# Eight of 22 feature blocks of the down projection as seven products in place of eight, with weight sums formed by adding transfers

## The chip, the cores and the metric

One core of one Trainium2 chip runs the whole layer. The metric is the device time of one execution in microseconds (us); lower is better. TensorE (PE) multiplies matrices, and its weight loads are shown apart as PEld. VectorE (DVE), ScalarE (ACT) and GpSimd (POOL) do elementwise work. SyncE (SP) and POOL issue the DMA transfers, each from a queue of its own.

## The reference

One decoder layer on 256 tokens with 2048 features, in float32:

```python
h = rmsnorm(x, attn_norm_g)
proj = h @ w_in                      # split among two attention groups
x = x + concat([o_mla, o_nsa]) @ w_o
h = rmsnorm(x, ffn_norm_g)
x = x + (silu(h @ w_gate) * (h @ w_up)) @ w_down   # 5632 hidden features
return rmsnorm(x, final_norm_g)
```

The change concerns the product with `w_down`, a 5632 x 2048 matrix: 44 blocks of 128 hidden features by 4 groups of 512 output columns.

## The kernel before

**Weights.** A class `Stream` brings every weight tile of 128 x 1024 from HBM, in the order in which PE uses them. `_dma` issues the load from SP's queue into one of three buffers (`wraw`). `_split` makes two parts of it: ACT casts it to a rounded copy `whi` (line 142), and DVE subtracts that from the tile to get the rest, `wlo` (line 144). While `W.share` is 256, in the attention stage and the output projection, POOL subtracts the last 256 columns (line 146) and DVE the first 768. Each of `whi` and `wlo` has three buffers, and `get` splits up to two tiles ahead of the one that PE uses. A product of two split operands takes three matmuls: high by high, high by low, low by high.

**The feed-forward stage.** The 44 feature blocks are worked in two halves of 22 (`h` is 0 or 1). For each block, `gate_up` multiplies two tiles of the gate and two of the up weights, 128 features at a time, into two PSUM banks (tags `ds` and `PT`, two buffers each). `activate` turns them into the split activation `aT`: copies by ACT, additions by DVE, one multiplication by POOL, the SiLU by ACT.

Then the half's down projection runs over four column groups `dg`. For each, 11 tiles of two feature blocks are multiplied with token half 0 and token half 1 into two banks (`down`, lines 863 to 865); one tile is 12 matmuls of 512 columns:

```python
for k in range(2):
    nc.tensor.matmul(pt, h_, wh, ...)   # activation high, weight high
    nc.tensor.matmul(pt, h_, wl, ...)
    nc.tensor.matmul(pt, l_, wh, ...)
```

After each group, DVE adds the two banks to `x`.

**The end.** In the last group (`h` 1, `dg` 3) the last four weight tiles are held back for token half 1. Token half 0 is added, normalized and stored while PE works the held tiles in two column halves of 256 (banks `dnh0`, `dnh1`; 48 matmuls of 256 columns). After the last of them come an addition of 256 columns by DVE, a sum of squares by ACT, a small reduction, a power by POOL, the scaling by DVE and ACT, and four stores by SP.

**Order of instructions.** PE executes in the order of the program text (`program()` writes it out by hand). The other engines and the DMA queues get an order that a planner makes from its estimates when the kernel is built: among the instructions whose inputs and buffers are free by the plan, the earlier in the text goes first. Where a wait is needed, a queue waits in that order.

Of the kernel before, what the change touches and what calls it, by code (L numbers as in the profile page):

```python
# [30 lines left out]
NSA_SCALE = 0.125  # L31


def program():
# [45 lines left out]
    for h in range(2):  # L80
        for f in range(h * NFH, (h + 1) * NFH):
            if f == 0:
                s += w(("gate", 0, 0), ("up", 0, 0)) + [("tp", 3)] + w(("gate", 1, 0), ("up", 1, 0))
                s += [("rb2",)] + w(("gate", 0, 1), ("up", 0, 1), ("gate", 1, 1), ("up", 1, 1))
            elif f > 1:
                s += w(*A("gate", f), *A("up", f))
        s += [("w", ("down", h, dg, j)) for dg in range(4) for j in range(NFH // 2)]
    return s


def plan():

    return [k[1] for k in program() if k[0] == "w"]
# [6 lines left out]
class Stream:  # L100
# [3 lines left out]
    SPLIT_AHEAD = 2  # L104

    def __init__(self, nc, pool, order, src):
        self.nc, self.pool, self.order, self.src = nc, pool, order, src
        self.raw, self.done = {}, {}
        self.nd = self.ns = self.nu = 0
        self.cuts = {0: (0, 368, G1W), 1: (0, 368, G1W)}  # L110
        self.apart = {}
        self.share = 0

    def _dma(self, upto):
        while self.nd < min(upto, len(self.order)):
            i = self.nd
            w = width(self.order[i])
            t = self.pool.tile([P, 1024], F32, tag="wraw", name=f"wraw{i}", bufs=self.DMA_AHEAD)
            cut = self.cuts.get(i, (0, w))
            for c0, c1 in zip(cut, cut[1:]):  # L120
                self.nc.sync.dma_start(t[:, c0:c1], self.src(i)[:, c0:c1])
            self.raw[i] = t
            self.nd += 1

    def _split(self, upto):
        nc = self.nc
        while self.ns < min(upto, len(self.order)):
            i = self.ns
            self._dma(i + 1)
            raw = self.raw.pop(i)  # L130
            if self.order[i][0] in ("w1k", "w1v"):
                self.done[i] = raw
            else:
                w = width(self.order[i])
                if i in self.apart:
                    hi, lo = (self.apart[i].tile([P, 1024], F32R, name=f"w{n}{i}") for n in ("hi", "lo"))
                else:
                    hi, lo = (self.pool.tile([P, 1024], F32R, tag=f"w{n}", name=f"w{n}{i}", bufs=3)
                              for n in ("hi", "lo"))
                cut = self.cuts.get(i, (0, w))  # L140
# [9 lines left out]
    def get(self, key):  # L150
        i = self.nu
        assert self.order[i] == key, (self.order[i], key)
        self.nu += 1
        self._dma(i + self.DMA_AHEAD)
# [5 lines left out]
def layer_kernel(ctx: ExitStack, tc: tile.TileContext, a: dict, out: bass.AP):  # L160
# [9 lines left out]
    W = Stream(nc, wp, order, wsrc)  # L170
# [20 lines left out]
    ssq = cp.tile([P, 2, 2, 5], F32, name="ssq")  # L191
    gates = cp.tile([P, 2, 48], F32, name="gates")
    oT = cp.tile([P, 16, 2, S], F32R, name="oT")
# [35 lines left out]
    ap = att.enter_context(tc.tile_pool(name="att", bufs=1))  # L229

# [31 lines left out]
    for k in range(KD):  # L262
# [24 lines left out]
        if k == 14:  # L287
# [7 lines left out]
            nc.vector.tensor_reduce(ssq[:, 1, :, 0], ssq[:, 0, :, 0:4], axis=AX.X, op=ALU.add)  # L295
# [512 lines left out]
    nc.vector.tensor_reduce(ssq[:, 1, :, 0], ssq[:, 0, :, 0:4], axis=AX.X, op=ALU.add)  # L808
# [4 lines left out]
    aT = fp.tile([P, NFH, 2, S], F32R, name="aT")  # L813
    gfin = fp.tile([P, D], F32, name="gfin")
    nc.gpsimd.dma_start(gfin, a["gfin"])
    W.apart = {len(order) - 2: fp, len(order) - 1: fp}

    def next_weights(*key):
        assert next(steps) == ("w", key)
        return W.get(key)  # L820

    def activate(h, f):

        t2 = fp.tile([P, 2, S], F32, tag="t2", name=f"t2_{h}_{f}", bufs=2)
        u = fp.tile([P, 2, S], F32, tag="gu", name=f"u_{h}_{f}", bufs=2)
# [7 lines left out]
        nc.vector.tensor_mul(u[:, 1, :], sl, u[:, 1, :])  # L833
        split(aT[:, f, 0, :], aT[:, f, 1, :], u[:, 1, :])

    for h in range(2):
# [11 lines left out]
        for dg in range(4):  # L848
            if dg % 2 == 0:
                dn = bank2(f"dn{h}_{dg}")  # L850
                pts = [dn[:, 0, :], dn[:, 1, :]]
            else:
                pts = [bank("S0", f"dn{h}_{dg}_0"), bank("O", f"dn{h}_{dg}_1")]
            last = h == 1 and dg == 3
            ntile = NFH // 2

            def down(t, j, w, pt, first, end, c=slice(0, 512)):
                hi, lo = w
                for k in range(2):
                    f = 2 * j + k  # L860
                    wh, wl = (v[:, k * 512 + c.start:k * 512 + c.stop] for v in (hi, lo))
                    h_, l_ = aT[:, f, 0, t * P:(t + 1) * P], aT[:, f, 1, t * P:(t + 1) * P]
                    nc.tensor.matmul(pt, h_, wh, start=f == 2 * first, stop=False)  # L863
                    nc.tensor.matmul(pt, h_, wl, start=False, stop=False)  # L864
                    nc.tensor.matmul(pt, l_, wh, start=False, stop=f == 2 * end - 1)  # L865

            def add(t, c0, c1, pt, i):

                xs = x[:, t, c0:c1]
                nc.vector.tensor_add(xs, xs, pt)  # L870
                if h == 1:
                    sq = fp.tile([P, 512], F32, tag="sq", name=f"fsq{t}{c0}", bufs=2)
                    nc.scalar.activation(sq[:, 0:c1 - c0], xs, AF.Square, scale=D ** -0.5,
                                         accum_out=ssq[:, 0, t, i:i + 1])

            def scale(t, *parts):

                r = rstd[:, 0, t:t + 1]
                for c0, c1, both in parts:
                    xv = x[:, t, c0:c1]  # L880
                    if both:
                        nc.vector.scalar_tensor_tensor(xv, xv, r, gfin[:, c0:c1], op0=ALU.mult, op1=ALU.mult)
                    elif c0 == 512:
                        nc.scalar.activation(xv, xv, AF.Copy, scale=r)
                    else:
                        nc.vector.tensor_scalar(xv, xv, r, None, op0=ALU.mult)
                    nc.sync.dma_start(out[0, t * P:(t + 1) * P, c0:c1], xv)

            def weigh(t, c0, c1):
                xs = x[:, t, c0:c1]  # L890
                nc.gpsimd.tensor_mul(xs, xs, gfin[:, c0:c1])

            keep = ntile - 4 if last else ntile
            held = []
            for j in range(ntile):
                w = next_weights("down", h, dg, j)
                down(0, j, w, pts[0], 0, ntile)
                if j >= keep:
                    held.append((j, w))
                else:  # L900
                    down(1, j, w, pts[1], 0, keep)
            cs = dg * 512
            if not last:
                for t in range(2):
                    add(t, cs, cs + 512, pts[t], dg)
                    if h == 1:
                        weigh(t, cs, cs + 512)
                continue
            add(0, cs, cs + 512, pts[0], 3)
            nc.vector.tensor_reduce(ssq[:, 1, 0, 1:2], ssq[:, 0, 0, 0:4], axis=AX.X, op=ALU.add)  # L910
            nc.vector.tensor_scalar(rstd[:, 0, 0:1], ssq[:, 1, 0, 1:2], EPS, None, op0=ALU.add)
            nc.gpsimd.tensor_tensor(rstd[:, 0, 0:1], rstd[:, 0, 0:1], half[:, 0:1], op=ALU.pow)
            x1 = x[:, 1, cs:cs + 512]
            nc.vector.tensor_add(x1, x1, pts[1])
            scale(0, (0, 512, False), (512, 1024, False), (1024, 1536, False), (1536, 2048, True))
            for b in range(2):
                pt = bank("PT", f"dnh{b}")[:, 0:256]
                for j, w in held:
                    down(1, j, w, pt, keep, ntile, slice(b * 256, (b + 1) * 256))
                add(1, cs + b * 256, cs + (b + 1) * 256, pt, 3 + b)  # L920
                if b == 0:
                    weigh(1, cs, cs + 256)
                    nc.vector.tensor_reduce(ssq[:, 1, 1, 1:2], ssq[:, 0, 1, 0:4], axis=AX.X, op=ALU.add)
# [131 lines left out]
```

## Time and profile before

| what | value |
|---|---|
| median of 3 runs | 1075.76 us (1074.13 to 1076.43) |
| the profiled execution's own time | 1075.57 us |
| span of the profile, first to last instruction | 1073.8 us |
| PE busy | 1052.7 us, 98% |
| DVE busy | 652.9 us, 61% |
| ACT busy | 565.8 us, 53% |
| POOL busy | 207.5 us, 19% |
| bytes moved by DMA | 193.57 MB, mean 180 GB/s |

The profile is one execution. Busy time counts instructions of an engine, and matmuls overlap in the pipeline, so the distance from one start to the next says what a matmul costs. The granted clock is that of TensorE, 1.00 for 2.4 GHz and 0.50 for 1.2 GHz. The DMA share is the mean busy share of the core's 16 DMA engines.

### The profile page before, as it was taken

To read this page: it belongs to the slowest core of one execution; us is meant where nothing else is said; L and a number is where in the kernel's file an instruction comes from. 1 tells how busy PE (TensorE), PEld (TensorE's weight loads), DVE (VectorE), ACT (ScalarE), POOL (GpSimd) and SP (SyncE) were. 2 spreads that over 40 slices of the span, in tenths; PEclk is the share of its full clock that TensorE was granted. 3 is DMA by queue.
4 is the path that set the end of the run, shared out by engine and by line. 5 is a ranking of instruction groups with operands and counts; after the bars stand their busy time and mean duration, and the time that the engine had idled before them with its cause. 6 is when DMAs were issued, how large, how long until landed. Compare 5 with 4: busy or idle time off the path is not lost.

```text
span 1073.8 us, 16240 instructions
## 1 busy us (share of the span) xinstructions
PE 1052.7 (98%) x6126; PEld 923.7 (86%) x6126; DVE 652.9 (61%) x1004; ACT 565.8 (53%) x996; POOL 207.5 (19%) x209
## 2 busy tenths in 40 slices
PE   8999999899999999999999999999999999999997
PEld 8999999788888888888888888888888888888886
DVE  5678989875656555555555454455555555555554
ACT  5768888754455545545444333345454454444442
POOL 2244446433342101001010000001010010101110
PEclk9999999999999999999999999999999999999998
DMA  8854343334456555555555555555555555555553
GB/s 278 281 168 159 119 133 105 99 105 151 136 178 216 182 192 193 183 193 187 188 194 185 193 193 194 196 194 183 192 189 186 194 184 189 195 186 190 195 194 137
DMA packets 54831, 193.57 MB, mean 180 GB/s; under 512 B 6436, under 2 KB 7076, under 8 KB 54624
## 3 DMA queue, kind: packets, MB, share of 16 engines
q1 hardware_dynamic: 54288, 191.36, 53.6%
q0 software_dynamic: 464, 1.17, 0.3%
q8 instruction: 48, 0.79, 0.3%
q14 instruction: 31, 0.25, 0.1%
HBM read 190.41 MB, written 2.10 MB: 179 GB/s over the span
## 4 chain that ended last, share of the span: by engine, by line
PE 90%; DVE 3%; DMA 3%; ACT 1%; POOL 1%; issue 1%; SPq 0%; POOLq 0%; DVEq 0%; ACTq 0%
PE up L798 15%; PE gate L798 15%; PE gate L801 8%; PE up L801 8%; PE dn L863 7%; PE dn L864 7%; PE dn L865 7%; PE woM L743 1%; PE woM L744 1%; PE woM L745 1%; PE woN L745 1%; PE woN L743 1%; PE woN L744 1%; PE ps_q L213 1%; PE ps_q L214 1%; PE ps_q L215 1%
## 5 line engine op out<-in xcount | busy, mean ns | idle before, releaser
L144 DVE TENSOR_TENSOR wlo<-wraw,whi 128x1024 fp32r<-128x1024 f32 (+3 forms) x352 | 421.1, 1197 | 376.1 <-ACT whi L142 374.8
L142 ACT CAST whi<-wraw 128x1024 fp32r<-128x1024 f32 (+2 forms) x352 | 366.4, 1041 | 438.7 <-PE dn L865 126.7
L798 PE MATMUL gate<-h2T,whi 128*128 128x512 f32 x704 | 221.2, 396 | 0.0
L798 PE MATMUL up<-h2T,whi 128*128 128x512 f32 x704 | 221.1, 395 | 0.0
L831 POOL TENSOR_TENSOR u<-t,RB 128x512 f32<-128x512 f32 x44 | 57.1, 1298 | 554.0 <-DVE t L830 554.0
L801 PEld LDWEIGHTS up<-h2T,wlo 128*128 128x128 f32 x704 | 132.3, 188 | 31.3
L801 PEld LDWEIGHTS gate<-h2T,wlo 128*128 128x128 f32 x704 | 132.2, 188 | 31.2
L801 PE MATMUL gate<-h2T,wlo 128*128 128x256 f32 x704 | 138.3, 278 | 0.0
L801 PE MATMUL up<-h2T,wlo 128*128 128x256 f32 x704 | 138.3, 278 | 0.0
L863 PE MATMUL dn<-whi,aT 128*128 128x512 f32 x344 | 133.8, 389 | 0.0
L864 PE MATMUL dn<-wlo,aT 128*128 128x512 f32 x344 | 133.8, 389 | 0.0
L865 PE MATMUL dn<-whi,aT 128*128 128x512 f32 x344 | 133.8, 389 | 0.0
L146 POOL TENSOR_TENSOR wlo<-wraw,whi 128x256 fp32r<-128x256 f32 x70 | 88.7, 1267 | 127.0 <-ACT whi L142 113.4
L798 PEld LDWEIGHTS gate<-h2T,whi 128*128 128x128 f32 x704 | 107.3, 189 | 0.2
L798 PEld LDWEIGHTS up<-h2T,whi 128*128 128x128 f32 x704 | 107.2, 189 | 0.0
L865 PEld LDWEIGHTS dn<-whi,aT 128*128 128x128 f32 x344 | 64.6, 188 | 13.5
L863 PEld LDWEIGHTS dn<-whi,aT 128*128 128x128 f32 x344 | 64.6, 188 | 13.4
L864 PEld LDWEIGHTS dn<-wlo,aT 128*128 128x128 f32 x344 | 64.6, 188 | 13.1
L213 PE MATMUL ps_q<-hT,whi 128*128 128x256 f32 x128 | 37.5, 293 | 0.5 <-ACT RB L209 0.5
L214 PE MATMUL ps_q<-hT,whi 128*128 128x256 f32 x128 | 36.2, 283 | 0.0
L215 PE MATMUL ps_q<-hT,wlo 128*128 128x256 f32 x128 | 36.2, 283 | 0.0
L743 PE MATMUL woN<-whi,oT 128*128 128x512 f32 x64 | 26.6, 415 | 0.0
(335 smaller groups left out, 1517.7 us busy)
## 6 DMA issues: line engine op xcount, KB each, us to landing
wraw<-in_w_dram SPq DMA_DIRECT2D x338, 512.0 KB, 3.4
wraw<-in_g_dram SPq DMA_DIRECT2D x14, 440.0 KB, 5.3
x<-in_x_dram SPq DMA_DIRECT2D x4, 512.0 KB, 7.0
xt<-in_xT_dram SPq DMA_DIRECT2D x3, 512.0 KB, 6.0
out_dram<-x SPq DMA_DIRECT2D x5, 256.0 KB, 2.5
gfin<-in_gfin_dram POOLq DMA_DIRECT2D x1, 1024.0 KB, 6.0
out_dram<-x SPq DMA_DIRECT2D x2, 320.0 KB, 2.7
wraw<-in_g_dram SPq DMA_DIRECT2D x2, 256.0 KB, 4.2
```

What stands on the lines that cost most here:

```text
L142: nc.scalar.copy(hi[:, c0:c1], raw[:, c0:c1])
L144: nc.vector.tensor_sub(lo[:, c0:c2], raw[:, c0:c2], hi[:, c0:c2].bitcast(F32))
L146: nc.gpsimd.tensor_sub(lo[:, c2:c1], raw[:, c2:c1], hi[:, c2:c1].bitcast(F32))
L213: nc.tensor.matmul(ps, hi, act[:, 0, :], start=start, stop=False)
L214: nc.tensor.matmul(ps, hi, act[:, 1, :], start=False, stop=False)
L743: nc.tensor.matmul(pts[t], h_, wh, start=first, stop=False)
L798: nc.tensor.matmul(pt, hi[:, kk * P:(kk + 1) * P], h2T[:, k], start=k == 0, stop=False)
L801: nc.tensor.matmul(pt[:, 0:S], lo[:, kk * P:(kk + 1) * P], h2T[:, k, 0, :], start=False, stop=k == KD - 1)
L831: nc.gpsimd.tensor_mul(u, t2, RB[:, None, :].to_broadcast([P, 2, S]))
L863: nc.tensor.matmul(pt, h_, wh, start=f == 2 * first, stop=False)
L864: nc.tensor.matmul(pt, h_, wl, start=False, stop=False)
L865: nc.tensor.matmul(pt, l_, wh, start=False, stop=f == 2 * end - 1)
```

## The change

**Seven products.** In each half, the first 8 of the 22 feature blocks go in two steps (`NS = 2`) of four blocks. A step views the activations as a 2 x 2 matrix of blocks (two token halves by two pairs of feature blocks) and the weights as one (two pairs of feature blocks by two column groups of 512). Seven products in place of eight give the four results: the activation side uses A11, A12, A22 and four sums or differences S1 to S4, and the weight side uses B11, B22, B21 and four sums: P1 = B11+B12, P3 = B12+B22, P2 = P1+B22, P4 = P2+B21. A product is six matmuls of 512 columns. It is done for two pairs of column groups (`p` is 0 or 1), so there are eight steps in all. The other 14 blocks of a half stay as they were ("plain" tiles, 14 per `p`), and are put between the products. The order in one `p` is

```
B11 p P1 p P3 p P2 p B22 p P4 p B21 | B11 p P1 p P3 p P2 p B22 p P4 B21 p p p
```

where `p` stands for a plain tile. All eight PSUM banks are in use in a down stage.

**Weight sums.** P1 and P3 are each formed by a load from SP's queue into a `wraw` buffer and a second transfer from POOL's queue that adds to the same buffer. P2 and P4 add one more tile each to the buffer of P1, after the buffer's previous content has been split. The plain tiles and B11, B22, B21 use six buffers of their own in the feed-forward stage (three before).

**Activations.** For the first 8 blocks `activate` forms S1 to S4 with four small DVE operations for each pair and splits all seven forms into `aS`.

**Combination.** After the last product of a `p`, `combine` spreads banks 1, 5, 6 and 7 over the four parts of `x` (one ACT copy, four DVE and four POOL operations), and at the end of the `p` DVE adds banks 2, 4, 3 and 8.

**Other edits.** `_split` no longer gives POOL a share; the second weight tile of the kernel is no longer loaded and split in two pieces; the gate banks of the second half are `S0` and `O`; `gfin` is loaded when the second half's down stage begins, into the buffer of `h2T`; `oT` moves to the attention pool. At the end three plain tiles are held for token half 1, and they go in whole banks of 512 columns; the final scaling goes in four parts of 512 columns for both token halves.

```diff
+NS = 2
+UNITS = ("B11", "P1", "P3", "P2", "B22", "P4", "B21")
+PLAIN = (2, 4), (3, 8)
+PRODUCT = {"B11": (A11, 1), "P1": (S1, 5), "P3": (S3, 7), "P2": (S2, 6), "B22": (S4, 3), "P4": (A22, 4), "B21": (A12, 2)}
...
+    SUM_AHEAD = 9
...
-        self.cuts = {0: (0, 368, G1W), 1: (0, 368, G1W)}
+        self.cuts = {0: (0, 368, G1W)}
...
+            elif u[1] in ("P1", "P3"):
+                x, y = ("B11", "B12") if u[1] == "P1" else ("B12", "B22")
+                t = self.pool.tile([P, 1024], F32, tag="wraw", name=f"{u[1]}_{self.na}", bufs=3)
+                nc.sync.dma_start(t, self.src(self._tile(u, x)))
+                nc.gpsimd.dma_start(t, self.src(self._tile(u, y)), accum_op=ALU.add)
...
+                before = self.units.index(("sw", {"P2": "P1", "P4": "P2"}[u[1]]) + u[2:])
+                if self.ns <= before:
+                    return
+                nc.gpsimd.dma_start(self.chain, self.src(self._tile(u, {"P2": "B22", "P4": "B21"}[u[1]])),
+                                    accum_op=ALU.add)
...
-                    c2 = c1 - self.share
-                    nc.vector.tensor_sub(lo[:, c0:c2], raw[:, c0:c2], hi[:, c0:c2].bitcast(F32))
-                    if c2 < c1:
-                        nc.gpsimd.tensor_sub(lo[:, c2:c1], raw[:, c2:c1], hi[:, c2:c1].bitcast(F32))
+                    nc.vector.tensor_sub(lo[:, c0:c1], raw[:, c0:c1], hi[:, c0:c1].bitcast(F32))
...
-            st[n, f] = bank("ds" if n == "gate" else "PT", f"{n}{f}")
+            tag = "PT" if n == "up" else "ds" if f < NFH else ("S0", "O")[f % 2]
+            st[n, f] = bank(tag, f"{n}{f}")
...
+    W.raws = (fp, "raw", 6)
...
+        nc.vector.tensor_sub(s1, a22, a21)
+        nc.vector.tensor_sub(s3, a11, a21)
+        nc.vector.tensor_add(s2, a11, s1)
+        nc.vector.tensor_sub(s4, a12, s2)
+        dst = aS[:, f // 4, f % 2]
+        split(dst[:, 0, A11, :], dst[:, 1, A11, :], a11)
+        split(dst[:, 0, A12:A22 + 1, :], dst[:, 1, A12:A22 + 1, :], two.rearrange("p (b s) -> p b s", b=2))
+        split(dst[:, 0, S1:, :], dst[:, 1, S1:, :], c)
...
+        if h == 1:
+            gfin = hp.tile([P, D], F32, tag="big", name="gfin")
+            nc.gpsimd.dma_start(gfin, a["gfin"])
...
+            def combine():
+                e, u, v, w = (temp(f"e{n}_{h}{p}") for n in range(4))
+                nc.scalar.copy(e, m[1])
+                nc.gpsimd.tensor_add(x11, x11, e)
+                nc.vector.tensor_sub(u, e, m[6])
+                nc.vector.tensor_add(w, u, m[5])
+                nc.gpsimd.tensor_sub(x12, x12, w)
+                nc.vector.tensor_add(u, u, m[7])
+                nc.vector.tensor_add(v, u, m[5])
+                nc.gpsimd.tensor_add(x21, x21, u)
+                nc.gpsimd.tensor_sub(x22, x22, v)
...
+                    mms(to, w, lambda k: [aS[:, i, k, b, form, :] for b in range(2)])
+                    if unit[1] == "B21" and i == NS - 1:
+                        combine()
+                    continue
+                plain(0, unit[1], w)
+                if end and n >= len(todo) - 3:
+                    held.append((unit[1], w))
+                else:
+                    plain(1, unit[1], w)
...
+            final(0, (2 * p, 2 * p + 1))
             for b in range(2):
...
+                for key, w in held:
+                    if key[2] % 2 == b:
+                        plain(1, key, w)
+                nc.vector.tensor_add((x21, x22)[b], (x21, x22)[b], m[4 if b == 0 else 8])
+                final(1, (2 * p + b,))
```

## Rows read from the trace of the kernel before

**Rows 1.** The profile's page: busy time, share and instructions of each engine

```profile
PE 1052.7 (98%) x6126; PEld 923.7 (86%) x6126; DVE 652.9 (61%) x1004; ACT 565.8 (53%) x996; POOL 207.5 (19%) x209
```

**Rows 2.** The page: the chain that ended last, by engine

```profile
PE 90%; DVE 3%; DMA 3%; ACT 1%; POOL 1%; issue 1%; SPq 0%; POOLq 0%; DVEq 0%; ACTq 0%
```

**Rows 3.** Groups of instructions, down stage of half 0 (busy, mean ns | idle)

```profile
L144 DVE TENSOR_TENSOR wlo<-wraw,whi 128x1024 fp32r<-128x1024 f32 x44 | 53.9, 1225 | 60.6 <-ACT whi L142 60.6
L142 ACT CAST whi<-wraw 128x1024 fp32r<-128x1024 f32 x44 | 46.4, 1055 | 72.4 <-PE dn L865 69.3 <-PE up L798 1.7 <-issue 1.4
```

**Rows 4.** Stretches: length, PE, PEld, DVE, ACT, POOL, clock, DMA share, GB/s

```profile
20.00:40.00 20.00, 19.89 (x170) 19.68 (x168) 10.94 (x16) 14.21 (x30) 1.11 (x5) 1.00 0.94 325
580.80:700.40 119.60, 119.60 (x530) 99.08 (x529) 58.66 (x54) 47.37 (x47) 1.30 (x1) 1.00 0.59 194
```

**Rows 5.** Timeline of the kernel's end (start, length, instruction, idle before)

```profile
1059.94 0.28 PE L863 MATMUL dnh<-whi,aT 128*128 128x256 f32 x1
...
1060.14 0.69 DVE L870 TENSOR_TENSOR x<-x,dn 128x512 f32<-128x512 f32 x1 [2.61 <-PE dn L865]
...
1060.87 0.63 ACT L873 ACTIVATE fsq<-x 128x512 f32<-128x512 f32 x1 [4.67 <-DVE x L870]
...
1063.42 0.74 DVE L882 SCALAR_TENSOR_TENSOR x<-x,rstd,gfin 128x512 f32<-128x512 f32 x1
...
1065.58 0.28 PE L865 MATMUL dnh<-whi,aT 128*128 128x256 f32 x1
1065.89 0.42 DVE L870 TENSOR_TENSOR x<-x,dnh 128x256 f32<-128x256 f32 x1 [0.47 <-PE dnh L865]
1066.41 0.42 ACT L873 ACTIVATE fsq<-x 128x256 f32<-128x256 f32 x1 [1.36 <-DVE x L870]
...
1066.95 0.16 DVE L926 TENSOR_TENSOR rstd<-ssq 128x1 f32<-128x1 f32 x1 [0.63 <-ACT fsq L873]
...
1067.78 0.95 DVE L886 TENSOR_SCALAR x<-x,rstd 128x512 f32<-128x512 f32 x2 [0.67 <-POOL rstd L927]
1068.64 0.48 DVE L882 SCALAR_TENSOR_TENSOR x<-x,rstd,gfin 128x256 f32<-128x256 f32 x1
```

**Rows 6.** DMA issues: queue, count, size of one, median us to landing

```profile
wraw<-in_w_dram SPq DMA_DIRECT2D x338, 512.0 KB, 3.4
...
x<-in_x_dram SPq DMA_DIRECT2D x4, 512.0 KB, 7.0
...
out_dram<-x SPq DMA_DIRECT2D x5, 256.0 KB, 2.5
gfin<-in_gfin_dram POOLq DMA_DIRECT2D x1, 1024.0 KB, 6.0
```

**Rows 7.** Groups of instructions on DVE, attention stage, 80 to 180 us

```profile
L144 DVE TENSOR_TENSOR wlo<-wraw,whi 128x768 fp32r<-128x768 f32 x24 | 27.0, 1127 | 2.7 <-ACT whi L142 2.3
```

**Rows 8.** Timeline of DVE in the attention stage: line 471 twice

```profile
175.65 2.14 DVE L471 TENSOR_SCALAR e<-e,ls 128x256 f32<-128x256 f32 x2
...
191.42 0.62 DVE L471 TENSOR_SCALAR e<-e,ls 128x256 f32<-128x256 f32 x2
```

**Rows 9.** Waits of PE, 0 to 345 us: total, times, longest

```profile
PE o L512 <- DVE pl L498: 2.6, 1, 2.6
```

**Rows 10.** Timeline of the start: the second weight tile's last piece

```profile
8.94 0.69 DVE L144 TENSOR_TENSOR wlo<-wraw,whi 128x512 fp32r<-128x512 f32 x1 [0.90 <-ACT whi L142]
```

**Rows 11.** Timeline: one weight tile's split in the down stage

```profile
1041.11 1.05 ACT L142 CAST whi<-wraw 128x1024 fp32r<-128x1024 f32 x1 [1.66 <-PE dn L865]
...
1042.20 1.22 DVE L144 TENSOR_TENSOR wlo<-wraw,whi 128x1024 fp32r<-128x1024 f32 x1 [0.67 <-ACT whi L142]
```

**Rows 12.** The page, costliest groups: POOL's operation of 128 x 512

```profile
L831 POOL TENSOR_TENSOR u<-t,RB 128x512 f32<-128x512 f32 x44 | 57.1, 1298 | 554.0 <-DVE t L830 554.0
```

**Rows 13.** Timeline of POOL around 337 us

```profile
337.26 0.65 POOL L815 DMA_DIRECT2D gfin<-in_gfin_dram  x1 [6.30 <-ACT sq L233]
337.93 0.73 POOL L203 TENSOR_TENSOR rstd<-rstd,half 128x2 f32<-128x2 f32 x1
```

More of the change, by code (lines that the diff above doesn't have):

```diff
@@ L86, in program, with loads @@
                 s += w(*A("gate", f), *A("up", f))
-        s += [("w", ("down", h, dg, j)) for dg in range(4) for j in range(NFH // 2)]
+        s += [u for p in range(2) for u in down_units(h, p)]
     return s
+def loads(step):
+    if step[0] == "w":
+        return [step[1]]
+    if step[0] == "sw" and step[1] in LOADS:
+        u, h, p, i = step[1:]
+        return [("down", h, 2 * p + TILES[n][1], 2 * i + TILES[n][0]) for n in LOADS[u]]
+    return []
 def plan():
-    return [k[1] for k in program() if k[0] == "w"]
+    return [k for s in program() for k in loads(s)]
 def width(key):
@@ L125, in _split @@
     def _split(self, upto):
         nc = self.nc
[L127 to L131, printed above, removed]
+        while self.ns < min(upto, len(self.units)):
+            i, u = self.ns, self.units[self.ns]
+            self._sum(i + 1)
+            n, raw = self.parts.pop(i)
+            self.live.discard(n)
+            if u[0] in ("w1k", "w1v"):
                 self.done[i] = raw
@@ L133, in _split @@
             else:
[L134 to L140, printed above, removed]
+                w = width(u) if u[0] != "sw" else 1024
+                hi, lo = (self.pool.tile([P, 1024], F32R, tag=f"w{m}", name=f"w{m}{i}", bufs=3) for m in ("hi", "lo"))
@@ L847, in layer_kernel @@
                 done += 1
[L848 to L857, printed above, removed]
+        W.DMA_AHEAD = 6
+        if h == 1:
+            gfin = hp.tile([P, D], F32, tag="big", name="gfin")
+            nc.gpsimd.dma_start(gfin, a["gfin"])
@@ L858, in down @@
                 hi, lo = w
+                first, last = count[to] == 0, count[to] == total[to] - 1
+                count[to] += 1
                 for k in range(2):
[L860 to L870, printed above, removed]
-                if h == 1:
[L872 to L902, printed above, removed]
@@ L913, in layer_kernel @@
-            x1 = x[:, 1, cs:cs + 512]
-            nc.vector.tensor_add(x1, x1, pts[1])
-            scale(0, (0, 512, False), (512, 1024, False), (1024, 1536, False), (1536, 2048, True))
-            for b in range(2):
[L917 to L923, printed above, removed]
-                    nc.vector.tensor_scalar(ssq[:, 1, 1, 1:2], ssq[:, 1, 1, 1:2], EPS, None, op0=ALU.add)
@@ new lines, in mms, with plain @@
+                    nc.tensor.matmul(m[to], l_, wh, start=False, stop=last and k == 1)
+            def plain(t, key, w):
+                f = 2 * key[3] - 4 * NS
+                mms(PLAIN[key[2] % 2][t], w, lambda k: [aN[:, f + k, b, t * P:(t + 1) * P] for b in range(2)])
+            def combine():
[9 more added lines that the diff above has]
+                nc.gpsimd.tensor_sub(x22, x22, v)
@@ new lines, in layer_kernel @@
+            end = h == 1 and p == 1
+            held = []
+            for n, unit in enumerate(todo):
+                assert next(steps) == unit
+                w = W.get(unit[1] if unit[0] == "w" else unit)
+                if unit[0] == "sw":
+                    form, to = PRODUCT[unit[1]]
+                    i = unit[4]
+                    mms(to, w, lambda k: [aS[:, i, k, b, form, :] for b in range(2)])
[5 more added lines that the diff above has]
+                    held.append((unit[1], w))
+                else:
+                    plain(1, unit[1], w)
```

166 lines of the change are left out of this document (126 added, 40 removed).

## The prediction

> **What bounds the kernel now.** I read the page first. PE is busy for 1052.7 of 1073.8 us [rows 1], and 90% of the chain that ended last is PE [rows 2]. A busy PE need not be a fast one, so I went to the stretch that changes. In the down stage of half 0 PE has no idle time, and the tile splits of ACT and DVE wait for PE rather than the other way round: the casts idle 72.4 us, 69.3 of them for a buffer that PE still reads [rows 3]. The clock is at 1.00, which is 2.4 GHz, and the DMA engines are 59% busy [rows 4]. So this stage lasts as long as its matmuls: 528 of them (11 tiles of 12 for four groups) in 119.6 us, 0.2265 us each [rows 4]. A matmul less is worth that, as long as weights keep coming.
>
> **Matmuls removed.** Before there are 1032 matmuls of 512 columns (176 in each of three lines for half 0, 168 for half 1, where 8 a line are cut in two) and 48 of 256. After, one `p` has 14 products of 6 and 14 plain tiles of 12, which is 252, and four times that is 1008. So 24 of 512 columns go, 24 x 0.2265 = 5.4 us, and all 48 of 256. These start from 1059.94 to 1065.58 us [rows 5]: 47 steps of 0.120, so 5.8 us. Together **-11.2 us**.
>
> **The end.** After the last matmul the addition covers 512 columns instead of 256 (0.69 for 0.42), and so does the sum of squares (0.63 for 0.42). A reduction and a scaling of about 0.16 each stand where one such operation stood; the last DVE scaling is two operations of 0.74, overlapping a little, where a pair of 0.95 and one of 0.48 stood; the last store is 256 KB, landing in 2.5 us [rows 5, 6]. That is 0.27 + 0.21 + 0.2 + 0.1 = **+0.8 us**. Token half 0's finish (two additions, two squares, scaling) takes some 4 us and lies beside the 18 held matmuls, 18 x 0.2265 = 4.1 us. If it overruns, the overrun adds to the end: 0 to 0.7, one addition; I take 0.
>
> **The attention stage.** POOL's share goes, so DVE subtracts 1024 columns instead of 768. A split of 768 takes 1.127 us there, and one of 1024 takes 1.225 in the down stage [rows 3, 7]: 24 x 0.1 = 2.4 us more DVE work in 100 us. Against that, DVE operations stretch in this stage: the same pair at line 471 takes 2.14 us once and 0.62 us another time [rows 8]. If POOL's subtractions cause such stretches, two fewer pay for all of it. DVE sets PE's longest wait after the start, 2.6 us [rows 9], so either sign can reach PE. Bounds: -2 to +2 us; I take 0, since the work added equals about two such stretches.
>
> **The start.** The second tile in one piece delays its low part. Its last piece ended at 8.94 + 0.69 = 9.63 us [rows 10]; whole, the cast and the subtraction are some 0.3 and 0.4 us longer. The first piece's issue is saved. Bounds 0 to 0.7; I take **+0.2**.
>
> **Forms and combination.** Per half, four pairs of blocks need small DVE operations and larger splits, about 6 us of DVE spread over the 245 us of the gate and up stage, and DVE is busy 61% of the whole [rows 1]. Per `p`, `combine` and four additions are 8 x 0.69 = 5.5 us of DVE, and 28 splits are 34.3: 40 of 57.1 us, so DVE has room. A product lasts 6 x 0.2265 = 1.36 us and a plain tile 2.72. The split of a tile takes 2.31 us, from the cast's start at 1041.11 to the subtraction's end at 1043.42 [rows 11]. Buffers let it run during the two units before; the shortest such pair is two products, 2.72 us, so 0.4 is spare. Four POOL additions come before the last DVE additions, 1.3 us each by POOL's operation of that size [rows 12], and three plain tiles (8.2 us) cover them. An adding transfer that waits in POOL's queue would hold them back; without the cover the next `p` waits up to 1.3 us, at three borders: 0 to 4 us. I take **+0.6**.
>
> **The weight sums.** This is the unknown. Per `p`, SP loads 20 tiles and the first parts of 4 sums, and POOL issues 8 adding transfers: 32 transfers of 512 KB in 252 x 0.2265 = 57.1 us. At 325 GB/s with a share of 0.94 [rows 4], full use is 346 GB/s, or 1.52 us for one. So they take 48.6 us, 85%, if an add costs what a load does.
>
> P1 and P3 need nothing that PE makes, only a free buffer. The planner's queues move such a transfer ahead: the load of `gfin` stands after the power of line 203 in the text, and POOL issues it before [rows 13]. So I expect three sums formed before each half's down stage.
>
> P2 and P4 are chained. Three buffers let P1, two units after B11, be split from the step's start, so its split ends 2.31 us after it at the earliest. With L from there to the landed sum, P2's split ends at 4.62 + L, and P4's at 6.93 + 2L. PE wants P2 at 4.08 + 8.16 = 12.24 and P4 at 20.40, so a step is late by 2L - 13.47 once **L is over 6.74 us**.
>
> No transfer of before adds. From below: a load of 512 KB lands in 3.4 us, and POOL takes 0.65 to issue, so L = 4.05 and nothing is late. From above: four loads of 512 KB in the crowded first stretch took 7.0 us [rows 6], so L = 7.65, 1.8 us late a step, 14.6 over eight steps. The nearest row is `gfin`: POOL's queue, 128 partitions, and with 1 MB as many bytes as an add reads from both places. It landed in 6.0 us while loads ran [rows 6, 13]: L = 6.65, just in time. I take that and **+1.0 us** for scatter.
>
> The Trainium skill (DMA: Bandwidth & Descriptors, Anatomy of one DMA) gives 2.0 us plus bytes over 436 GB/s for POOL's transfers: an estimate of 4.4 for `gfin`, where the row has 6.0, so the measurement decides; by the page the chain would cost 0 and the sum be 1 us lower.
>
> **Sum**, against the profiled execution's 1075.57 us (span and what lies around it): -11.2 + 0.8 + 0.2 + 0.6 + 1.0 = -8.6, so 1067.0; the median of the three runs is 0.2 higher: **1067.2 us**.
>
> **Rival 1: the adds are slow, slower than before.** An add occupies the DMA engines for two loads' time. Then a `p` asks for 24 x 1.52 + 8 x 3.04 = 60.8 us of transfers in 57.1, the queues never empty, and L is 0.65 + 3.4 + 1.52 = 5.6 when alone and 8.6 when loads take every second packet. What is formed ahead (six tiles, three sums) softens the first. In the middle of the upper half, L = 7.9: 2.3 us late a step, 18.6 in all, **1086 us**; at 8.6 it is 30 us, 1097. It decides against the change from L = 7.3, where eight steps lose the 8.6 us won. For it: 85% leaves little room even with cheap adds, and a landing went from 3.4 to 7.0 us at 94% [rows 4, 6]. Against: `gfin`'s 6.0 us for as many bytes. Chance 0.33.
> The Trainium skill (Collectives: The Full Stack, The bandwidth ceiling) has such a rule: an adding transfer reads two sources through the same ring and so runs at about half a copy's rate. By that rule this rival is the outcome; no run here shows it yet.
>
> **Rival 2: the first sums come late.** If the queues keep the order of the text, P1 of each half is asked for only when B11 is, some 3 us before the stage. Load, add and split are 3.4 + 6.65 + 2.31 = 12.4 us, and PE wants P1 after 4.1: 5.3 us late, twice, +10.6, **1077.8 us**, no gain left. For: the text asks late. Against: [rows 13]. Chance 0.07.
>
> **Rival 3: small waits of all kinds.** Borders at 4, attention at 2, some chains late by 3: **1074 us**, no change. Chance 0.08.
>
> **How the numbers follow.** The forecast (1063 to 1072) has 0.52. 0.2% is about 2 us, what a measurement can tell from no change. Faster: the forecast and half of rival 3, 0.56. Same: 0.07, from rivals 2 and 3. Slower: rival 1 and part of rival 2, 0.37. The range goes from 1064 (attention 2 us better) to 1097 (L = 8.6): 0.04 below it, 0.12 above; the forecast's own is 1063 to 1072.
>
> **What would show it.** The down stage's matmuls: 1008 of 512 columns at 0.2265, none of 256, the two halves' stages about 114.2 us each. No wait of PE for a cast or subtraction at P2 and P4; if there is one, twice a step, the adds are to blame, and the landing of POOL's adding transfers says by how much: 6.0 by the forecast, over 6.7 by rival 1. A wait at the first P1 only would be rival 2. DMA share in the stage near 0.85 with cheap adds, near 1.0 with dear ones. The end after the last matmul is 0.8 us longer. PE's waits before 345 us should stay within 2 us of before. The prediction falls if L is not near 6, or if the queues hold POOL's other work behind an add that waits.

## The result, and the profile after

The changed kernel takes **1115.96 us** (median; 1112.82 to 1118.47) where the kernel before took 1075.2 beside it: a ratio of 1.0378, interval 1.0360 to 1.0397. The forecast was 1067.2, the range ended at 1097. It is slower by 40.8 us, and more than the slow rival allowed. In what follows one execution of run 2, 1150.7 us at a granted clock of 0.85 where its others have 0.99 and more, is left out of the median.

First the page of the changed kernel: busy time by engine, the DMA queues (packets, MB, share of 16 engines), the chain that ended last, and the DMA issues.

```profile
PE 1062.1 (95%) x6054; PEld 921.6 (83%) x6054; DVE 708.8 (64%) x1078; ACT 593.5 (53%) x1031; POOL 174.1 (16%) x184
...
q1 hardware_dynamic: 55296, 195.55, 52.5%
q0 software_dynamic: 5072, 17.95, 8.7%
...
PE 78%; DMA 10%; DVE 4%; ACT 3%; issue 3%; POOL 1%; SPq 0%; POOLq 0%; DVEq 0%; ACTq 0%
...
wraw<-in_w_dram SPq DMA_DIRECT2D x330, 512.0 KB, 4.2
P<-in_w_dram POOLq DMA_DIRECT2D x32, 512.0 KB, 8.5
...
gfin<-in_gfin_dram POOLq DMA_DIRECT2D x1, 1024.0 KB, 8.0
```

PE is left with 78% of the chain, for 90% [rows 2]; 10% is now DMA, and that share belongs to one tile, P, the weight sums. In the median an adding transfer lands 8.5 us after its issue. PE's busy time rose by 9 us [rows 1] though it has fewer matmuls, a first sign of slower ones.

The stages of the two halves, as stretches (length, PE, PEld, DVE, ACT, POOL, clock, DMA share, GB/s), and under them PE's waits in each (total, times, longest):

```profile
578.60:721.00 142.40, 124.99 (x506) 99.47 (x505) 79.02 (x74) 59.63 (x61) 27.68 (x25) 0.94 0.81 232
966.20:1106.20 140.00, 125.28 (x506) 99.06 (x504) 81.21 (x76) 63.44 (x75) 33.30 (x28) 0.94 0.70 199
```

```profile
PE m L997 <- ACT whi L225: 13.6, 5, 4.1
PE m L998 <- DVE wlo L226: 3.8, 6, 0.8
...
PE m L997 <- ACT whi L225: 10.1, 4, 4.7
PE m L998 <- DVE wlo L226: 4.3, 7, 0.8
```

The first stretch took 119.6 before [rows 4]. 504 matmuls at 0.2265 would be 114.2 each. From first matmul to last the two stages take 142.4 + 139.7 us, 53.7 longer than their matmuls, and two things share it. PE waits 17.4 + 14.4 = 31.8 us; counted from one matmul's start to the next, the steps with such a wait are 37.3 us longer than 0.2265 each, since a matmul lasts 0.39 us and only its overlap with the next makes a step of 0.2265. Another 81 steps without a wait last over 0.3 us, at a mean clock of 0.94: 15.7 us more. (PE's busy time, 250.3 us instead of 228.3, holds these 15.7 and the lost overlap.) Everything else nearly cancels. The first gate matmul starts at 332.31 us for 334.43, the gate and up stages are as long as before (246.3 and 245.2), and from the last matmul's end to the span's end there are 8.50 us for 7.94. Half 1's stage runs to 1105.90, the last matmul's end: 139.7 for 120.2. In sum: -2.1 + 22.7 + 19.5 + 0.6 = +40.7, and the spans differ by 40.6.

How the stage's groups have turned round (busy, mean ns | idle before) is seen beside [rows 3]: there the casts waited 69.3 us for PE. Here those of loaded tiles still wait for it, 29.8 us, but those of the sums wait 40.5 us for DMA, and PE waits for them.

```profile
L226 DVE TENSOR_TENSOR wlo<-wraw,whi 128x1024 fp32r<-128x1024 f32 x40 | 50.4, 1277 | 16.6 <-ACT whi L225 15.2
...
L225 ACT CAST whi<-wraw 128x1024 fp32r<-128x1024 f32 x40 | 41.4, 1050 | 29.8 <-PE m L999 29.8
...
L997 PE MATMUL m<-whi,aS 128*128 128x512 f32 x56 | 24.1, 431 | 13.6 <-ACT whi L225 13.6
...
L225 ACT CAST whi<-P 128x1024 fp32r<-128x1024 f32 x16 | 16.8, 1051 | 53.0 <-DMA P<-in_w_dram 40.5 <-PE m L999 10.7 <-PE up L881 1.7
```

**One late sum, step by step.** The timeline of half 0's first step (start, length, instruction, idle before it and what ended that). Line 206 issues the chained adds (P2, P4), line 198 those of P1 and P3:

```profile
579.73 1.23 DVE L226 TENSOR_TENSOR wlo<-P,whi 128x1024 fp32r<-128x1024 f32 x1 [1.56 <-ACT whi L225]
...
581.25 0.88 POOL L206 DMA_DIRECT2D P<-in_w_dram  x1 [9.66 <-DVE wlo L226]
...
588.13 1.22 DVE L226 TENSOR_TENSOR wlo<-P,whi 128x1024 fp32r<-128x1024 f32 x1 [1.09 <-ACT whi L225]
...
590.09 0.87 POOL L198 DMA_DIRECT2D P<-in_w_dram  x1 [6.41 <-DMA P<-in_w_dram]
590.67 1.19 POOL L206 DMA_DIRECT2D P<-in_w_dram  x1
...
601.00 1.04 ACT L225 CAST whi<-P 128x1024 fp32r<-128x1024 f32 x1 [7.50 <-DMA P<-in_w_dram]
...
602.09 0.49 PE L997 MATMUL m<-whi,aS 128*128 128x512 f32 x1 [2.89 <-ACT whi L225]
603.36 0.50 PE L998 MATMUL m<-wlo,aS 128*128 128x512 f32 x1 [0.77 <-DVE wlo L226]
...
604.00 0.63 PE L997 MATMUL m<-whi,aS 128*128 128x512 f32 x1
```

P1's split ends at 580.96, P2's add lands 5.4 us after its issue, at 586.65: L = 5.7, inside the prediction's budget of 6.74. P2's split ends at 589.35, but POOL issues P4's add only at 590.67. Ahead of it stands an add of line 198, P3 of the next step, which had itself waited for its first load. P4's add then takes 10.2 us to land, and the cast starts at 601.00: L = 11.6. The prediction's formula with the two values gives 5.7 + 11.6 - 13.47 = 3.8 us late; PE waits 2.89 + 0.77 = 3.7. After the wait the matmuls start 0.43 us apart instead of 0.2265 until 607 us.

The same place as stretches (columns as above). In the first PE runs out of weights, in the second it comes back:

```profile
595.00:601.00 6.00, 4.20 (x19) 3.16 (x17) 0.00 (x0) 0.00 (x1) 0.00 (x0) 1.00 1.04 287
601.00:607.00 6.00, 4.14 (x11) 3.01 (x12) 3.90 (x4) 3.99 (x4) 0.00 (x0) 0.74 0.53 186
```

While everyone waits for P4 the DMA engines are full (1.04) and move 287 GB/s; before, a share of 0.94 moved 325 [rows 4]. The granted clock then falls to 0.74 over 6 us, a stretch at 1.2 GHz in one at 2.4. Here ten steps between 603.36 and 607.34 take 3.98 us instead of 2.27: 1.7 us lost on top of the wait.

**When an add is late.** Of the sixteen chained adds, the five that are issued while no other transfer of POOL's queue is under way land in 5.2 to 5.5 us. The other eleven have one before them and land in 7.7 to 10.7. For P4 it is the next sum's add at seven of the eight steps; in half 1's first step P2's add stands behind the 1 MB of `gfin`, issued 2.2 us before it. In the very last step no sum is left to be moved ahead: P4's add, issued at 1084.56, lands in 5.3 us, at 1089.9; its cast starts when PE frees a buffer, and PE waits for no cast in this step.

```profile
1090.11 1.06 ACT L225 CAST whi<-P 128x1024 fp32r<-128x1024 f32 x1 [1.66 <-PE m L999]
```

**What an add costs the DMA engines** follows from the page. Queue q1 took 52.5% of 1114.4 us for 195.55 MB, which is 1.57 us of all sixteen engines for 512 KB. Queue q0 took 8.7%, 97.0 us; `gfin` and the small transfers at q1's rate are some 3.5 of it, so an add is 93.5 / 32 = 2.92 us, 1.9 loads.

### The profile page after: what moved, and what is told of

The parts are those of the page before. It is cut to its first block, busy times and chain, and to the rows that moved or that the text cites. A ratio compares the mean times of both kernels' runs of the same rounds, so it can differ in the third digit from the quotient of the medians.

```text
span 1114.4 us, 16221 instructions
## 1 busy us (share of the span) xinstructions
PE 1062.1 (95%) x6054; PEld 921.6 (83%) x6054; DVE 708.8 (64%) x1078; ACT 593.5 (53%) x1031; POOL 174.1 (16%) x184
## 3 DMA queue, kind: packets, MB, share of 16 engines
q1 hardware_dynamic: 55296, 195.55, 52.5%
## 4 chain that ended last, share of the span: by engine, by line
PE 78%; DMA 10%; DVE 4%; ACT 3%; issue 3%; POOL 1%; SPq 0%; POOLq 0%; DVEq 0%; ACTq 0%
PE up L881 15%; PE gate L881 15%; DMA P<-in_w_dram 10%; PE gate L884 7%; PE up L884 7%; PE m L998 4%; PE m L999 3%; PE m L997 3%; DVE wlo L226 2%; ACT whi L225 2%; PE woM L825 1%; PE woM L826 1%; PE woM L827 1%; PE ps_q L293 1%; PE woN L825 1%
## 5 line engine op out<-in xcount | busy, mean ns | idle before, releaser
L226 DVE TENSOR_TENSOR wlo<-wraw,whi 128x1024 fp32r<-128x1024 f32 (+2 forms) x343 | 426.8, 1248 | 281.0 <-ACT whi L225 277.1
L226 DVE TENSOR_TENSOR wlo<-P,whi 128x1024 fp32r<-128x1024 f32 x32 | 40.9, 1278 | 87.6 <-ACT whi L225 87.0
L998 PE MATMUL m<-wlo,aN 128*128 128x512 f32 x224 | 89.8, 401 | 0.8 <-DVE wlo L226 0.8
L997 PE MATMUL m<-whi,aN 128*128 128x512 f32 x224 | 90.1, 402 | 0.0
L999 PE MATMUL m<-whi,aN 128*128 128x512 f32 x224 | 88.8, 396 | 0.0
L225 ACT CAST whi<-P 128x1024 fp32r<-128x1024 f32 x32 | 33.6, 1051 | 100.1 <-DMA P<-in_w_dram 67.9
L997 PE MATMUL m<-whi,aS 128*128 128x512 f32 x112 | 48.0, 428 | 23.7 <-ACT whi L225 23.7
L998 PE MATMUL m<-wlo,aS 128*128 128x512 f32 x112 | 48.6, 434 | 7.4 <-DVE wlo L226 7.4
L998 PEld LDWEIGHTS m<-wlo,aN 128*128 128x128 f32 x224 | 43.8, 195 | 11.1 <-DVE wlo L226 1.7
L997 PEld LDWEIGHTS m<-whi,aN 128*128 128x128 f32 x224 | 43.8, 195 | 9.6
L999 PEld LDWEIGHTS m<-whi,aN 128*128 128x128 f32 x224 | 43.6, 195 | 9.4
L997 PEld LDWEIGHTS m<-whi,aS 128*128 128x128 f32 x112 | 22.6, 202 | 32.4 <-ACT whi L225 27.9
```

Source lines behind the costliest of these rows:

```text
L226: nc.vector.tensor_sub(lo[:, c0:c1], raw[:, c0:c1], hi[:, c0:c1].bitcast(F32))
L997: nc.tensor.matmul(m[to], h_, wh, start=first and k == 0, stop=False)
L998: nc.tensor.matmul(m[to], h_, wl, start=False, stop=False)
L999: nc.tensor.matmul(m[to], l_, wh, start=False, stop=last and k == 1)
```

## The experiments

Each ran beside the kernel before on the same chip (1074.4 to 1075.0 us). They are in the order in which they were made.

**1. No adding.**

```diff
-                nc.gpsimd.dma_start(t, self.src(self._tile(u, y)), accum_op=ALU.add)
+                nc.gpsimd.dma_start(t, self.src(self._tile(u, y)))
...
-                nc.gpsimd.dma_start(self.chain, ..., accum_op=ALU.add)
+                nc.gpsimd.dma_start(self.chain, ...)
```

> All 32 adding transfers become plain ones of the same size, on the same queue, into the same tiles and behind the same waits; the weight sums are left out, so the output is another. Theory A (an add is long because it also reads its destination): the landing falls from 8.5 us to about 4.5, so L = 0.9 + 4.5 = 5.4 lies under the 6.74 that the chain allows, PE's waits for whi and wlo in the two down stages fall from 32 us to under 4, and the time is 1064 to 1070 us. Theory B (POOL's queue: issue of 0.87 us and transfers that stand behind one another, whatever they do): the landing stays over 7 and the time over 1090. Theory C (too many transfers for the DMA engines): bytes written are the same, so the DMA share stays near 0.8 and the time over 1090.

Measured: 1071.2 us, ratio 0.9973 (0.9958 to 0.9988). The queue's share and line 206's durations (min/median/max) and landings:

```profile
q0 software_dynamic: 5072, 17.95, 5.0%
...
L206 POOL DMA_DIRECT2D P<-in_w_dram x16: 527/528/591, 580.4 to 1038.5; - x16
...
DMA to landing us min/median/max: 3.7/5.9/7.4
```

With the same bytes the queue takes 5.0% of 1066.6 us, by the same working 1.56 us a transfer: it is the adding that costs 1.9 times a load. POOL's issue is 0.53 us instead of 0.87. In this trace (an execution of 1068.6 us) PE doesn't wait for a cast in the down stages any more, only for subtractions:

```profile
PE m L997 <- DVE wlo L225: 2.9, 7, 0.6
```

Theories B and C fall, and A's outcome holds, though the landing is longer than it said (5.9 for 4.5) and the time 1 us over its range. That the reading of the destination is the reason is not shown by a run. The Trainium skill (Collectives: The Full Stack, The bandwidth ceiling) says of the adding step of a reduce-scatter that it reads two sources and so gets about half a copy's rate; the 2.92 and 1.56 us here agree with such a ratio.

**2. The chained adds alone, 3. the adds of P1 and P3 alone.**

```diff
 # 2
-                nc.gpsimd.dma_start(t, self.src(self._tile(u, y)), accum_op=ALU.add)
 # 3
-                nc.gpsimd.dma_start(self.chain, ..., accum_op=ALU.add)
```

> Only the 16 chained adds (P2, P4) stay; the adds of P1 and P3 are left out, so their tiles hold one block each and the output is another. Theory A with its own latency as the cause: a chained add alone took some 9 us to its landing (issued at 613.13, cast released at 622.10), so a step is still late by 2 x 9 - 13.5 = 4.5 us: 8 x 4.5 = 36 us less what loads in the way no longer cost, 1085 to 1105. Theory D (the chained add is late because another sum's add stands before it in POOL's queue): L falls to 6 or less, waits go, 1064 to 1072.

> Only the 16 adds of P1 and P3 stay; the chained adds are left out (P2 and P4 read the tile of P1 again), so the output is another. Theories A and D: without the chain nothing that PE waits for is asked for late, so no wait for whi in the down stages and 1064 to 1070 us. Theory C (adds load the DMA engines, loads come late): waits stay at about half, 1085 to 1100.

Measured: 1080.0 us (ratio 1.0048, 1.0029 to 1.0066) and 1067.0 (0.9930, 0.9915 to 0.9944). The landings of the chained adds in run 2, and PE's waits there:

```profile
DMA to landing us min/median/max: 5.3/6.0/9.0
```

```profile
PE m L997 <- DVE wlo L225: 7.1, 13, 0.8
...
PE m L996 <- ACT whi L224: 1.3, 3, 0.6
```

The adds that nothing waits for early cost nothing measurable: in run 3 PE waits for no cast in the down stages, and 2.5 us for subtractions. The chained ones alone cost some 13 us against run 3, less than theory A said and more than D. (The add at 613.13 from which theory A worked was not alone: the one issued at 607.51 landed at 617.75.) Six of the eight in half 0 land in 5.3 to 6.0 us, two, beside loads (the DMA share is 0.89 around the first), in 8.3 and 9.0. All eight adds of P4 land in 5.3 to 6.1 us here, for 8.7 to 10.7 at seven of the eight steps of the changed kernel. 13 us for one kind and none for the other do not add up to the 49 us between 1116.0 and 1067.0. About 36 us arise only where both kinds are there.

**4. All sums on DVE.**

```diff
-                nc.sync.dma_start(t, self.src(self._tile(u, x)))
-                nc.gpsimd.dma_start(t, self.src(self._tile(u, y)), accum_op=ALU.add)
...
+                self.ENGINE[u[1]](self.nc).tensor_add(t, self.chain if x is None else self.raw[b[x]], self.raw[b[y]])
```

`ENGINE` is DVE for all four sums. Each tile is now loaded once, in the order of use, a sum goes to a buffer of its own, and sums are formed four units ahead instead of nine (`SUM_AHEAD`).

> The same sums, formed by DVE from tiles that are loaded once: four additions of 1024 columns a step, each about 1.22 us by the split's subtraction; 22 transfers of 512 KB per p instead of 32, none on POOL. If the adding transfers alone are to blame: DVE is busy 40 + 8 x 1.22 = 50 of 57.1 us per p, no chain beyond DVE's queue, and the time is what the prediction gave without its sums, 1062 to 1068. Rival: DVE is now too full, the splits come late at products of 1.36 us (a sum and a split take 1.22 + 2.31 = 3.5 us), waits of 1 us at each of 32 sums, and the time is 1080 to 1095.

Measured: 1082.3 us (1.0053, 1.0034 to 1.0073). The time lies in the rival's range, but by another way than a DVE that is too full: PE waits 18 times, not 32. DVE's sums in half 0's down stage and PE's wait over the whole run:

```profile
L209 DVE TENSOR_TENSOR P<-P,wraw 128x1024 f32<-128x1024 f32 x7 | 9.4, 1348 | 4.2 <-DMA wraw<-in_w_dram 4.0
L209 DVE TENSOR_TENSOR P<-wraw,wraw 128x1024 f32<-128x1024 f32 x6 | 7.4, 1226 | 6.7 <-DMA wraw<-in_w_dram 6.6
```

```profile
PE m L1006 <- DVE wlo L234: 14.2, 18, 2.2
```

A sum whose load hasn't landed holds DVE's queue (10.6 us in this stage), and the subtractions that PE waits for stand behind it.

**5. P4's add ahead of the next step's.** In each half, the first loads of P1 and P3 of the three later steps are held by a one-column copy:

```diff
+                if (u[3], u[4]) != (0, 0):
+                    nc.scalar.copy(t[:, 0:1], self.gate)
                 nc.sync.dma_start(t, self.src(self._tile(u, x)))
...
+                if u[:2] == ("sw", "P2"):
+                    self.gate = self.pool.tile([P, 1], F32, tag="gate", name=f"gate{i}", bufs=2)
+                    nc.scalar.copy(self.gate, hi[:, 0:1].bitcast(F32))
```

> The same 32 adds, in another order: the first load of P1 and P3 of each later step is held (by a copy of one column on ACT) until P2 of the step before is cast, so that P4's chained add stands ahead of the adds for the next step, not behind one. In the run with the chained adds alone they landed in 6.0 us, in the changed kernel in 8.8. Theory D (standing behind another sum's add makes the chain late): chained landings go to about 6 to 7, the long waits for whi at P4 go, and the time is 1070 to 1085. Theory A alone (an add is 2.9 us of the DMA engines wherever it stands, and the engines are simply short of time): no change, 1105 to 1118.

Measured: 1092.7 us (1.0161, 1.0139 to 1.0183), between the two. The timeline of POOL, and the stretches after P4's add:

```profile
588.85 0.88 POOL L208 DMA_DIRECT2D P<-in_w_dram  x1 [6.18 <-DVE wlo L228]
593.23 0.87 POOL L200 DMA_DIRECT2D P<-in_w_dram  x1 [3.51 <-ACT whi L227]
596.31 0.86 POOL L200 DMA_DIRECT2D P<-in_w_dram  x1 [2.21 <-DMA P<-in_w_dram]
```

```profile
593.00:598.00 5.00, 5.00 (x23) 4.04 (x22) 1.11 (x1) 0.35 (x1) 1.73 (x2) 1.00 1.06 288
598.00:604.00 6.00, 5.24 (x22) 3.74 (x21) 4.72 (x4) 3.64 (x4) 0.00 (x0) 1.00 1.04 270
```

P4's add is issued 0.3 us after the end of P2's subtraction instead of 1.3, and first in line. It lands in 8.7 us all the same, beside three loads that were issued within 1.1 us of it. Its first packet moves only at 592.64, 3.8 us after its issue, where it is 1.6 for an add with little beside it; why is open. Then the engines are full for 11 us with the adds for the next step. The median landing of the chained adds stays 8.8. The order was worth 23 us, so what stands ahead matters, but a place in POOL's queue is not all of it.

**6. P2 and P4 on DVE, P1 and P3 still by adding transfers.**

```diff
+                    nc.vector.tensor_add(self.chain, self.chain, raw)
...
-                nc.gpsimd.dma_start(self.chain, self.src(self._tile(u, {"P2": "B22", "P4": "B21"}[u[1]])),
-                                    accum_op=ALU.add)
```

`raw` is the tile of B22 or B21 that the product after the sum's needs anyway.

> P1 and P3 stay adding transfers; P2 and P4 are formed in place by DVE from the tile of P1 and the loaded B22 and B21, which their own products need anyway. 28 transfers of 512 KB per p instead of 32, half of the adds, no chain through the DMA queues; DVE has 4 x 1.22 = 4.9 us more per p. By theories A and D together: as the run without chained adds (1067.0 measured), plus at most 1 us for DVE: 1066 to 1070, faster than before. Rival (what cost the version with all sums on DVE 15 us was DVE's queue order and not its load): sums stand ahead of splits that PE waits for, 1072 to 1080.

Measured: **1067.7 us**, ratio 0.9935 (0.9923 to 0.9948): faster than both kernels, as expected. Its stages are 116.5 and 118.3 us at full clock, and DVE's group of sums is this:

```profile
577.50:694.00 116.50, 115.12 (x505) 94.24 (x505) 93.62 (x82) 60.82 (x61) 24.31 (x17) 1.00 0.79 242
939.20:1057.50 118.30, 115.71 (x506) 94.07 (x504) 95.88 (x84) 64.26 (x75) 30.67 (x20) 1.00 0.64 200
```

```profile
L203 DVE TENSOR_TENSOR P<-P,wraw 128x1024 f32<-128x1024 f32 x8 | 11.9, 1493 | 0.0
```

**7. The same on POOL** (`nc.gpsimd.tensor_add` in place of `nc.vector.tensor_add`).

> As the version before, but P2 and P4 are formed by POOL, 1024 columns in some 2.6 us (twice its 1.3 us for 512), so L is 2.6 us of the 6.74 allowed and DVE has no more work. If only the chain's length counts: 1066 to 1070. Rival: a POOL addition stands in POOL's queue behind an adding transfer that waits for its first load, as P4's add did in the changed kernel, or it slows DVE's subtractions: 1075 to 1100.

Measured: 1078.9 us (1.0041, 1.0026 to 1.0056). POOL's sums in half 0's down stage take 2.5 us, as thought; but here are DVE's subtractions of that stage in run 6 and, in the second fence, in run 7:

```profile
L232 DVE TENSOR_TENSOR wlo<-wraw,whi 128x1024 fp32r<-128x1024 f32 x40 | 52.7, 1329 | 13.0 <-ACT whi L231 11.4
```

```profile
L203 POOL TENSOR_TENSOR P<-P,wraw 128x1024 f32<-128x1024 f32 x8 | 20.4, 2545 | 27.9 <-DVE wlo L232 27.9
...
L232 DVE TENSOR_TENSOR wlo<-wraw,whi 128x1024 fp32r<-128x1024 f32 x39 | 63.7, 1648 | 15.9 <-ACT whi L231 14.8
```

A subtraction takes 1.65 us instead of 1.33: DVE is rid of the 11.9 us of sums and pays 11.0 in the longer subtractions of this group alone. Single subtractions show it: of the stage's 55, the 17 that overlap a POOL addition (a sum, or one of `combine`'s or `activate`'s) take 1.7 to 3.4 us, the other 38 take 1.21 to 1.23. Of the rival, its second half is seen (DVE is slowed); whether POOL's queue also held sums back wasn't separated. The Trainium skill (GPSIMD Engine Reference, Specifications) states that POOL's interfaces to SBUF are shared with VectorE, with contention for VectorE's instructions with two inputs there; these durations agree.

**8. The kernel before, with POOL's share alone removed.**

```diff
-    W.share = 256
+    W.share = 0
```

> The kernel before with one edit of the change alone: POOL takes no share of the subtractions of the attention stage. Theory: POOL's subtractions slow DVE, as the first gate matmul came 2.1 us earlier in the changed kernel (332.31 for 334.43), so the time falls by 1 to 2.5 us to a ratio of 0.998 to 0.999. Rival: those 2 us come from elsewhere (the order of the planner, the second tile in one piece), and this kernel is the same or 1 to 2 us slower.

Measured: 1073.1 us, ratio 0.9982 (0.9972 to 0.9993), a time as the theory said. The group that answers to [rows 7], and PE's wait that answers to [rows 9]:

```profile
L144 DVE TENSOR_TENSOR wlo<-wraw,whi 128x1024 fp32r<-128x1024 f32 x24 | 31.2, 1300 | 4.2 <-ACT whi L142 4.1
```

```profile
PE o L512 <- DVE pl L498: 0.9, 2, 0.5
```

Per subtraction DVE gives 0.17 us more for a third more columns, and PE's wait of 2.6 us is 0.9 (all of PE's waits before 345 us: 11.6 us for 13.0). The first gate matmul starts at 331.92, so a gain like the 2.1 us of the changed kernel comes with this edit alone. The mechanism is in part argued: in this trace a pair of line 471 still takes 2.69 us, and among the traces of the kernels without the share that start lies anywhere from 330.6 to 333.9.

**9. Plain neighbours.** The chained adds stay, P1's and P3's transfers don't add:

```diff
-                nc.gpsimd.dma_start(t, self.src(self._tile(u, y)), accum_op=ALU.add)
+                nc.gpsimd.dma_start(t, self.src(self._tile(u, y)))
```

> The 16 chained adds stay; the transfers of P1 and P3 stay in POOL's queue and in size, but don't add (the output is another). This tells a neighbour's place in POOL's queue from its adding. If POOL's queue is what holds the chained add: as the changed kernel, over 1100. If the DMA engines' time is what counts (an add 2.9 us, a plain one 1.6): P1's and P3's transfers take 16 x 1.3 us less of the engines, a chained add behind one lands in about 8 instead of 10.4 us, and the time lies between the run without adds in front (1081) and the changed kernel, at 1084 to 1095.

Measured: 1100.8 us (1.0242, 1.0225 to 1.0258), at the bound of the first theory and above what the second allowed. The pair of the timeline above, here:

```profile
591.13 0.59 POOL L198 DMA_DIRECT2D P<-in_w_dram  x1 [6.47 <-DMA P<-in_w_dram]
591.72 0.91 POOL L206 DMA_DIRECT2D P<-in_w_dram  x1
```

```profile
600.69 1.04 ACT L225 CAST whi<-P 128x1024 fp32r<-128x1024 f32 x1 [6.20 <-DMA P<-in_w_dram]
```

The chained add lands 8.9 us after its issue, and in 8.8 to 9.3 in the half's four such pairs. So a plain transfer in front costs a chained add some 3 us (5.3 to 6.1 for P4's adds in run 2), and its adding 1 us more (9.8 to 10.6 in the changed kernel's four pairs). In run 1, where neither adds, the second of such a pair took 4.8 to 6.1.

The trace also shows in what order the two passed. These are POOL's queue's packets (number, MB, share) from the neighbour's issue to its landing, 591.13 to 595.20 us, and from there to the add's landing at 600.59:

```profile
q0 software_dynamic: 144, 0.52, 44.1%
...
q0 software_dynamic: 144, 0.52, 51.8%
```

That is one whole transfer, then the other: the queue's order. The add took 5.4 us from its neighbour's landing, about as long as an add with little beside it takes here from its issue (5.1).

**10. One step instead of two** (`NS = 1`).

> The changed kernel with one Strassen step per pair of column groups instead of two (4 of 22 feature blocks): 12 matmuls less than before instead of 24 beside the last 48, 16 adds instead of 32. If each step loses the same: half of 54 us in the down stages, 27, and a gain of 8.5 from the rest: about 1094. If the loss is one step's adds and first loads on top of the other's chain: the steps now lie 57 us apart, only the first load of the next P3 is near, some 1.5 us a step remain, and the time is 1070 to 1080.

Measured: 1096.2 us (1.0189, 1.0164 to 1.0215): close to the first theory, so each step loses about the same, and distance between steps doesn't help. In its POOL timeline the next sum of line 198 again stands 0.59 us ahead of P4's add, since its first load is issued at 587.66, once P3's buffer is free, 62 us before its cast at 649.68.

## Why the prediction was wrong

**The step that failed is the weight sums' term**, "the nearest row is `gfin` ... just in time", +1.0 us. For a chained add with nothing else in its queue and few loads beside it, L is near that row or better: 5.7 for P2 in the timeline, and 5.2 to 5.5 from issue to landing for five of the sixteen, against the 6.0 taken (6.65 with the issue). What failed is the use of one L for all links. P4's add comes when the planner has just freed P3's buffer and moved the next sum's load and add ahead, so that POOL's queue has another transfer in front at seven of eight steps, and SP's loads fill the engines: L = 11.6 in the timeline. Four of P2's adds come behind a sum's add or `gfin` too. The term measures 37.3 us of waits.

**It had no price for the clock.** In the two stages TensorE's clock was at 1.2 GHz after the longer waits, and the matmuls at that level cost 15.7 us more. PE never waited in this stage before [rows 3], but the trace of before has such a place elsewhere: PE's wait of 2.6 us [rows 9] ended at 191.03, and the stretch behind it (columns as in [rows 4]) was at half clock, with 13 matmuls in it.

```profile
191.00:194.40 3.40, 3.37 (x13) 3.09 (x14) 2.78 (x8) 2.92 (x7) 1.80 (x3) 0.50 0.16 66
```

**Rival 1** had the premise right, an add is 2.92 us for 3.04 assumed, and the place (PE's waits for whi at the chained sums, with wlo after). Its price of 1086 to 1097 was too low, because it let a chained add share with loads only, not with the other sums, and left out the clock. Its other sign fails: the DMA share is 0.81 and 0.70, not near 1.0. The engines are full only in the stretches where a chained add runs and half idle after (1.04, then 0.53).

**Rival 2** is refuted: half 0's first three sums were formed from 347.09 us on, and half 1's had landed by 720.7, both well before their stages, as [rows 13] suggested. That same moving ahead is what put the wrong add in front later.

**The smaller terms.** Matmuls: the 1008 are there at 0.2265 where the clock is full and PE doesn't wait, so that term holds. Run 3's 1067.0 beside a forecast of 1067.2 is partly luck: its stages are 4.4 us over their matmuls, and its first gate matmul comes 2.2 us earlier than before, for which the forecast had nothing. End: +0.56 for +0.8. Attention: -1.7 alone in run 8, near the better bound, for 0. Start: the second tile's low part ended at 10.59 for 9.63 [rows 10], 0.96 late and over the bound of 0.7; PE waits 0.46 us for it, and its longest wait there, for the first cast, is 4.8 us for 5.0. Combination and borders: not separated from the sums in the changed kernel; in run 6 the stages are 6.5 us over 228.3 with sums and borders together.

**What the runs leave.** Run 1 against run 9 says that the chained adds' adding is worth 30 us; run 2 against run 9 that plain transfers of POOL's queue beside them are worth 21; run 9 against the changed kernel that their adding is worth 15 more. Two causes are seen: POOL's queue lets the transfer in front pass first (run 9's packets), and loads alone can make an add late (8.3 to 9.2 us in runs 2 and 5, at shares of 0.89 to 1.06). How the some 36 us divide between them is not shown.

## What to carry to other kernels

A chain of dependent transfers is priced link by link, each with what the queue and the engines will hold at its moment, and first of all what the planner moves ahead into the place that a link has just freed. A link forecast 0.1 us under its limit has no margin for that, and a wait of PE is to be priced with the slow matmuls behind it. Where a sum's addends are loaded anyway, a vector addition in the chain and adding transfers off it was the best split here: 1067.7 us, 0.65% under the kernel before and at the time that was forecast for the change.

## Not expected of the hardware

An adding transfer took 1.9 times a plain one's DMA time and 0.87 us of POOL to issue, for 0.53. The matmuls at the lower clock cost four tenths of what the waits before them did (15.7 and 37.3 us). POOL's additions lengthened DVE's subtractions from 1.33 to 1.65 us in the mean, and those beside a POOL sum to 2.3 to 3.4, so that moving eight sums a half to the idle engine cost 11 us (1078.9 for 1067.7).
